# A hybrid encoder block on one Trainium2 core: attention scores and outputs issued as blocks, weight casts put behind evictions, transposes placed later

## The chip, the cores and the metric

The kernel runs on one core of a Trainium2 chip. The metric is the device time of one execution in microseconds (us); three runs of the kernel before were taken, and their median is used. A core has a matrix engine (TensorE, "PE" in the profile; its weight loads are listed apart as "PEld"), a vector engine (DVE), a scalar engine (ACT), a general engine (POOL) and an engine that mostly issues transfers (SP). Each works through its own instructions in the order in which the program gives them, and waits on semaphores for the others.

## The reference

One layer of a hybrid streaming encoder, on 256 tokens of 1024 channels, in fp32: a feed-forward block (FFN), a mixer with two branches (HGRN2, a gated linear recurrence, and FoX, an attention with a forget gate), a read of a 256-token memory by four heads, and a second FFN. Cut to its core:

```python
h = rmsnorm(x, ffn1_pre_g);  x = x + 0.5 * rmsnorm(swiglu(h, ffn1_w_in, ffn1_w_down), ffn1_post_g)

h = rmsnorm(x, mix_pre_g)
q_a, f_a, i_a, g_a, q_b, k_b, v_b, f_b, gates = split(h @ w_in)
o_a = hgrn2_chunkwise(q_a, f_a, i_a, lb)            # recurrence, chunks of 64 tokens
o_a = rmsnorm(o_a, hg_norm_g) * silu(g_a);  y_a = o_a @ w_branch_a
o_b = fox_attention(q_b, k_b, v_b, f_b + bias)      # causal softmax, 128-query blocks
y_b = o_b @ w_branch_b
gate = sigmoid(gates + b_gate)
y = gate[0] * y_a + gate[1] * y_b
x = x + rmsnorm(y @ w_out, mix_post_g)

h = rmsnorm(x, mem_pre_g);  mem_n = rmsnorm(mem, mem_kv_g)
p = softmax(q @ k.T / 16)                           # q = h @ w_mq; k, v = split(mem_n @ w_mkv)
x = x + rmsnorm((p @ v) @ w_mo, mem_post_g)

h = rmsnorm(x, ffn2_pre_g);  x = x + 0.5 * rmsnorm(swiglu(h, ffn2_w_in, ffn2_w_down), ffn2_post_g)
```

## The kernel before

Everything is computed in products of fp32 parts. A weight unit of 128 x 1024 comes in by DMA as `raw`; `load_split` (lines 127 to 136) makes of it `hi` (a cast to fp32r on ACT, line 134) and `lo` (the rest, `raw - hi`, on DVE, line 135). Activations are held transposed in a `Pair` of the same two parts, `hT` and `lT`. A product is three matmuls per block: hi x hi, hi x lo, lo x hi. All matmuls are issued by the helper `MM` on line 90, so most rows of the profile carry that line, and are told apart by their tiles: `mm` (projections, 2 PSUM buffers), `acc` (accumulators, 4 buffers), `tr` (transposes and some small products, 2 buffers). `raw` has 4 buffers, `hi` and `lo` 8 each.

The stages follow each other in program order: FFN 1 (0 to 192 us in the profiled execution), the projections of the mixer with the recurrence (to 344), scores of FoX, its values v_b, outputs and gates, and the two branches (344 to 470), w_out (to 492), the memory read (to 599), FFN 2 (to 785). FFN and projections go through the weights in units of 4 per chunk; tokens come in two halves `h` of 128, and channels in blocks `kb` of 128.

A token-major result becomes a `Pair` through `to_T` (from line 279): eight transposes on PE into two `tr` buffers, four in each, and for every 128 x 128 block an eviction on ACT (`hT`, line 275) and one on DVE (`lT`, line 276). `half` does this for the normed `xs` of one half of the tokens. `split` (lines 152 to 154) makes the two parts from a PSUM tile without a gain.

The order of the engines' work is the program's order, but for blocks under `with after(i)`: they are given a high priority and may be issued only after the i-th matmul of the log. So a constant such as `L_IA = 36` says how many matmuls of the current stage go ahead of a block of transposes. `tc.issue_after` with one instruction does the same for a single transfer or cast. In this kernel those constants are:
- `L_ACT`, `L_F1`, `L_F2`: transposes of the FFN's gated activations (`flush`, line 359) and of the next input;
- `L_IA`, `L_MO`: transposes of `xs` for the second half, in i_a and around the memory output;
- `L_OA`, `F_T`, `F_O`: in the FoX stage, the transposes of the gated HGRN2 output `Gt` into the pair `OA` among v_b, the transposes of the probabilities (`fox_pT`, line 885) and the two outputs (`fox_out`);
- `M_O`: the first two memory outputs.

In the FoX stage the scores of both groups `g` of four heads come first (`fox_scores(0)`, `fox_scores(1)`), then the values, then the first chunk of gates, among which the transposed probabilities and the outputs are placed; further gates follow after the norm of the memory. The scores take their PSUM from `tr` (h = 0) and `acc` (h = 1). In the memory read the scores and the transposes of the probabilities stand between `mem_v(0)` and `mem_v(1)`.

The functions that the change touches, with the line numbers of the profile:

Of the kernel before, what the change touches and what calls it, by code (L numbers as in the profile page):

```python
# [11 lines left out]
F32 = mybir.dt.float32  # L12
F32R = mybir.dt.float32r
I32 = mybir.dt.int32
AF = mybir.ActivationFunctionType
# [3 lines left out]
P = 128  # L19
# [14 lines left out]
STAG = 3  # L34

L_ACT = 21
L_F1 = 24
L_IA = 36
L_WO = 28
L_MK = 108  # L40
L_MO = 21
L_F2 = 44
L_OA = 20
F_T = (8, 26)
F_O = (27, 42)
L_Y = 16
M_O = (24, 36)

R_AT = (52, 126, 210, 254, 298, 344)

# [25 lines left out]
def block_kernel(ctx: ExitStack, tc: tile.TileContext, wts, head_in, gf_in, x_in, mem_in, memT_in, cols, rows, fbias, masks, out):  # L76
# [23 lines left out]
    def nm(s):  # L100
        count[0] += 1
        return f"{s}_{count[0]}"
# [13 lines left out]
    def trp():  # L116
        return pp.tile([P, 512], F32, tag="tr", name=nm("tr"), bufs=2)
# [2 lines left out]
    cache = {}  # L120
    loads = []

    def parts_of():
        return [wp.tile([P, D], F32R, tag=t, name=nm(t), bufs=8) for t in ("hi", "lo")]

    def load_split(src, n=512):

        raw = wp.tile([P, D], F32, tag="raw", name=nm("raw"), bufs=4)
        hi, lo = parts_of()
        r, h, l = raw, hi, lo  # L130
        if n < 512:
            r, h, l = (p.rearrange("p (k n) -> p k n", k=2)[:, :, :n] for p in (raw, hi, lo))
        loads.append(nc.sync.dma_start(r, src).ins)
        S.copy(h, r)  # L134
        V.tensor_tensor(out=l, in0=r, in1=h.bitcast(F32), op=ALU.subtract)  # L135
        return hi, lo

    def unit(name, i):
# [5 lines left out]
    def chunk(name, c):  # L144
        return [unit(name, 4 * c + i) for i in range(4)]
# [4 lines left out]
        return hi[:, o : o + n], lo[:, o : o + n]  # L150

    def split(hi, lo, src):
        S.copy(hi, src)
        V.tensor_tensor(out=lo, in0=src, in1=hi.bitcast(F32), op=ALU.subtract)

    class Pair:

# [112 lines left out]
    def gain_split(X, kb, src, g, a=0, b=T, first=False):  # L270
        gs = cols_s[:, g + kb : g + kb + 1] if isinstance(g, int) else g
        if first:
            V.tensor_scalar(out=X.hi(kb, a, b), in0=src, scalar1=gs, scalar2=None, op0=ALU.mult)
        else:
            S.activation(X.hi(kb, a, b), src, AF.Copy, scale=gs)  # L275
        V.scalar_tensor_tensor(out=X.lo(kb, a, b), in0=src, scalar=gs, in1=X.hi(kb, a, b).bitcast(F32), op0=ALU.mult, op1=ALU.subtract)  # L276

    def to_T(X, src, h, g, qs=(0, 1)):

# [64 lines left out]
    def ffn(w_in, w_dn, X, r2, n_tok, i_row, first_half, second_half=None):  # L344
# [48 lines left out]
        def down(c, h, cols=((0, 512), (512, 1024))):  # L393
            act = acts[c]
            hs = slice(h * P, (h + 1) * P)
            for j in range(2):
                wh, wl = unit(w_dn, 2 * c + j)
                ah, al = act[:, 0, j, hs], act[:, 1, j, hs]
                for lo, up in cols:
                    for i, (a, w) in enumerate(((ah, wh), (ah, wl), (al, wh))):  # L400
                        MM(accs[h][lo // 512][:, lo % 512 : lo % 512 + up - lo], a, w[:, lo:up], start=(c == 0 and j == 0 and i == 0), stop=(c == NFF - 1 and j == 1 and i == 2))
# [19 lines left out]
        for c in range(n_tok, NFF):  # L421
            acts[c] = m4([P, 2, 2, T], F32R, "act")
            if c == 2 and first_half:
                n = len(log)
                (outs,) = act_first((c,), mm)
                for h in range(2):
                    flush(n + L_ACT + 24 * h)
                    act_evac(outs[h], c, h)
            else:
                for h in range(2):  # L430
                    n = len(log)
                    act_tok(c, h)
                    if c == 2 or c > NFF - STAG + 1:
                        flush(n + L_ACT)
            if c == 6:
                grow = load_row(i_row)
                if first_half:
                    with tc.issue_after(loads[-1]):
                        nc.sync.dma_start(masks_s, masks)
            if accs is None:  # L440
                accs = [[acc(), acc()], [acc(), acc()]]
            while done < min(c - 1, NFF - STAG):
                n = len(log)
                for h in range(2):
                    down(done, h)
                flush(n + L_ACT)
                done += 1
        left, right = (0, 512), (512, 1024)
        m = len(log)
        for cut in (left, right):  # L450
            for c in range(NFF - STAG, NFF):
                down(c, 0, (cut,))
        flush(m + L_ACT)
        post(accs[0], 0, grow, 0.5, not first_half)
        m = len(log)
        if first_half:
# [69 lines left out]
    for h in range(2):  # L526
        m = len(log)
        for c in range(2):
            ps = mm()
            proj_tok(ps, X2, chunk("i_a", c), h)  # L530
            iv_last = S.activation(iv[c][:, h, :], ps, AF.Copy, scale=r2[h]).ins
        if h == 0:
            half(X2, r2, 1, G_MIX, m + L_IA, into=fac_of(0, 1))
# [313 lines left out]

    ps_, pT0s, pT1s = {}, [], []

    def fox_scores(g):  # L850
        k, q = kb_[g], qb_[g]
        for h in range(2):
            ns = P * (h + 1)
            if h == 0:
                pv = trp().rearrange("p (i s) -> p i s", i=4)
                pv = [pv[:, i] for i in range(4)]
                p = sp.tile([P, 4, P], F32, tag="z2", name=nm("p0"), bufs=3)
            else:
                pv = score_psum()
                p = m4([P, 4, T], n="p1")  # L860
            mx, sm = s1(4, name="mx"), s1(4, name="sm")
            for i in range(4):
                MM(pv[i], q[:, i, h * P : (h + 1) * P], k[:, i, :ns], start=True, stop=True)
            for i in range(4):
                hd = 4 * g + i
                c1 = ct[:, h * 8 + hd : h * 8 + hd + 1]
                if h == 1:
                    V.scalar_tensor_tensor(out=p[:, i, 0:P], in0=pv[i][:, 0:P], scalar=c1, in1=cbc[:, hd], op0=ALU.add, op1=ALU.subtract)
                ds_ = slice(h * P, (h + 1) * P)
                V.scalar_tensor_tensor(out=p[:, i, ds_], in0=pv[i][:, ds_], scalar=c1, in1=cbm[g][:, i, ds_], op0=ALU.add, op1=ALU.subtract)  # L870
            V.tensor_reduce(out=mx, in_=p, axis=AX.X, op=ALU.max, negate=True)
            for i in range(4):
                S.activation(p[:, i], p[:, i], AF.Exp, bias=mx[:, i : i + 1], accum_out=sm[:, i : i + 1])
            V.reciprocal(sm, sm)
            V.tensor_tensor(out=p, in0=p, in1=bc(sm, [P, 4, ns], 2), op=ALU.mult)
            ps_[g, h] = p

    def fox_pT(g):
        pT0 = m4([P, 4, T], n="pT0")
        pT1 = sp.tile([P, 4, P], F32, tag="pT1", name=nm("pT1"), bufs=1)  # L880
        for h in range(2):
            for b in range(h + 1):
                tr = trp()
                for i in range(4):
                    PE.transpose(tr[:, i * P : (i + 1) * P], ps_[g, h][:, i, b * P : (b + 1) * P], ident)  # L885
                trv = tr.rearrange("p (i s) -> p i s", i=4)
                if b == 0:
                    S.copy(pT0[:, :, h * P : (h + 1) * P], trv)
                else:
                    V.tensor_copy(pT1, trv)  # L890
        pT0s.append(pT0)
        pT1s.append(pT1)
# [13 lines left out]
            i2 = slice(2 * j, 2 * j + 2)  # L906
            split(OB.h[g][:, i2], OB.l[g][:, i2], po.rearrange("p (a t) -> p a t", a=2))

    fox_scores(0)
    fox_scores(1)  # L910
    for c in range(2):
        u = chunk("v_b", c)
        t = m4([P, 2, 512], n="v_b")
# [2 lines left out]
            proj_tok(ps, X2, u, h)  # L916
            S.activation(t[:, h, :], ps, AF.Copy, scale=r2[h])
        vb_.append(t)
    for h in range(2):
        with after(len(log) - L_OA * (2 - h)):  # L920
            to_T(OA, lambda kb: Gt[h][:, kb * P : (kb + 1) * P], h, G_HG)


    zs = []
# [12 lines left out]

    m = len(log)
    gates(0)
    for g in range(2):  # L940
        with after(m + F_T[g]):
            fox_pT(g)
        with after(m + F_O[g]):
            fox_out(g)


# [10 lines left out]
        rm.append(rstd_x([ms[:, 0:512], ms[:, 512:]], fac_of(1, h)))  # L957

    rowm = row_of(fac[1])
    for c in range(1, 4):  # L960
        gates(c)
    for c in (0, 2, 1, 3):
        S.activation(zs[c], zs[c], AF.Sigmoid)
# [74 lines left out]
    def mem_v(c):  # L1038
        u = chunk("mv", c)
        VM.more()  # L1040
        for h in range(2):
# [4 lines left out]
            S.activation(vh, ps, AF.Copy, scale=rm[h])  # L1046
            V.scalar_tensor_tensor(out=vl, in0=ps, scalar=rm[h], in1=vh.bitcast(F32), op0=ALU.mult, op1=ALU.subtract)

    mem_v(0)
    pT = Pair()  # L1050
    for h in range(2):
        a, b = h * P, (h + 1) * P
        sc = s1(name="sc")
        V.tensor_scalar(out=sc, in0=r3[h], scalar1=1.0 / 16.0, scalar2=None, op0=ALU.mult)
# [13 lines left out]
            S.activation(p[:, i], pv[i], AF.Exp, bias=mx[:, i : i + 1], scale=sc, accum_out=sm[:, i : i + 1])  # L1068
        V.reciprocal(sm, sm)
        V.tensor_tensor(out=p, in0=p, in1=bc(sm, [P, 4, T], 2), op=ALU.mult)  # L1070
        for sb in range(2):
            tr = trp()
            for i in range(4):
                PE.transpose(tr[:, i * P : (i + 1) * P], p[:, i, sb * P : (sb + 1) * P], ident)  # L1074
            split(pT.h[sb][:, :, a:b], pT.l[sb][:, :, a:b], tr.rearrange("p (i s) -> p i s", i=4))
    g3 = load_row(2)
    AO = Pair()

# [12 lines left out]
        i2 = slice(2 * (i % 2), 2 * (i % 2) + 2)  # L1091
        split(AO.h[i // 2][:, i2], AO.l[i // 2][:, i2], ps.rearrange("p (a t) -> p a t", a=2))

    m = len(log)
    mem_v(1)
    for i in range(2):
        with after(m + M_O[i]):
            mem_out(i)
    for i in range(2, 4):
        mem_out(i)  # L1100
    X4 = Pair()
    r4 = [None, None]
    po = [[acc(), acc()], [acc(), acc()]]
# [107 lines left out]
```

## Time and profile before

| | |
|---|---|
| Time, median of 3 runs | 794.03 us (793.59 to 794.23) |
| Time of the profiled execution | 793.74 us |
| Its span (first to last recorded instruction) | 791.3 us |
| Mean granted clock of TensorE | 0.998 of full speed |
| Busy DVE, ACT, POOL | 519.0, 426.6, 14.1 us |
| DMA | 147.82 MB, 187 GB/s mean |

Times of the trace count from the start of the span. An instruction of PE counts as busy from its start, also while it waits in the array for its operand, and consecutive matmuls overlap, so lengths of pieces and distances of starts are read, not the sum of durations. "x24" behind a row is the number of instructions in it. A row of the timeline ends with the idle time before it and what released it, where there was any.

### The profile page before, as it was taken

Reading aid. Unit: us, or ns where it says so; the run is one execution under the profiler, and the core shown is the slowest. Engines: PE = TensorE matmul, PEld = TensorE weight load, DVE = VectorE, ACT = ScalarE, POOL = GpSimd, SP = SyncE. Lnnn points to the kernel's source line nnn. Section 1 sums busy time; section 2 is a strip of 40 time slices with the busy share of each in tenths; the row PEclk is TensorE's granted clock in tenths of the full one; section 3 lists DMA queues with packets and bytes.
Section 4 is the critical chain, followed back from the end, with each engine's and each line's share of the span. In section 5 each row is a group of like instructions: output and inputs, shape, how many; then the busy total and the mean of one; then the engine's idle time right before and its main releaser. Section 6 shows DMA issues by size and latency. Waiting matters only on the chain.

```text
span 791.3 us, 12219 instructions
## 1 busy us (share of the span) xinstructions
PE 783.2 (99%) x4736; PEld 678.0 (86%) x4736; DVE 519.0 (66%) x826; ACT 426.6 (54%) x656; POOL 14.1 (2%) x36
## 2 busy tenths in 40 slices
PE   9999999999999999999999999999999999999996
PEld 7888888887899999998888888999888888888885
DVE  6775545557767899498685666966649754545543
ACT  7654444546754667368674345645637644444541
POOL 0000000000000102100000000000000000000000
PEclk9999999999999999999999999999999999999999
DMA  9786654554554547735576654556433656654521
GB/s 349 251 259 203 231 191 160 190 208 161 165 188 143 181 134 224 257 121 173 168 257 222 212 188 161 166 191 201 144 122 133 227 196 207 214 194 159 186 80 54
DMA packets 44345, 147.82 MB, mean 187 GB/s; under 512 B 5048, under 2 KB 8768, under 8 KB 44288
## 3 DMA queue, kind: packets, MB, share of 16 engines
q1 hardware_dynamic: 43168, 144.83, 54.1%
q0 software_dynamic: 688, 1.85, 0.9%
q8 instruction: 37, 0.61, 0.3%
q10 hardware_dynamic: 432, 0.37, 0.1%
q14 instruction: 20, 0.16, 0.1%
HBM read 145.97 MB, written 1.06 MB: 186 GB/s over the span
## 4 chain that ended last, share of the span: by engine, by line
PE 97%; DVE 1%; issue 0%; DMA 0%; ACT 0%; DVEq 0%; ACTq 0%
PE mm L90 67%; PE acc L90 27%; PE tr L359 1%; PE tr L284 1%; PE tr L90 1%; DMA head<-in_head_dram 0%; PE tr L885 0%; DVE lo L135 0%; PE tr L972 0%; PE tr L1074 0%; DVE xs L340 0%; ACT hi L134 0%; DVE G L831 0%; DVE q_b L789 0%; DVE post L330 0%
## 5 line engine op out<-in xcount | busy, mean ns | idle before, releaser
L135 DVE TENSOR_TENSOR lo<-raw,hi 128x1024 fp32r<-128x1024 f32 (+1 forms) x256 | 306.4, 1206 | 124.2 <-ACT hi L134 115.5
L134 ACT CAST hi<-raw 128x1024 fp32r<-128x1024 f32 (+1 forms) x256 | 262.4, 1038 | 151.5 <-PE mm L90 86.5
L90 PE MATMUL mm<-lo,hT 128*128 128x512 f32 (+1 forms) x592 | 227.1, 386 | 0.0
L90 PE MATMUL mm<-hi,hT 128*128 128x512 f32 (+1 forms) x592 | 226.8, 385 | 0.0
L90 PE MATMUL mm<-hi,lT 128*128 128x512 f32 (+1 forms) x592 | 226.3, 386 | 0.0
L90 PEld LDWEIGHTS mm<-hi,hT 128*128 128x128 f32 x592 | 111.2, 188 | 21.9 <-ACT hT L275 0.6
L90 PEld LDWEIGHTS mm<-hi,lT 128*128 128x128 f32 x592 | 111.1, 188 | 21.8 <-DVE lT L276 0.5
L90 PEld LDWEIGHTS mm<-lo,hT 128*128 128x128 f32 x592 | 111.0, 188 | 20.5
L90 PE MATMUL acc<-hi,act 128*128 128x512 f32 x352 | 111.9, 390 | 0.0
L90 PE MATMUL mm<-hT,lo 128*128 128x256 f32 x384 | 109.0, 284 | 0.0
L90 PE MATMUL mm<-hT,hi 128*128 128x256 f32 x384 | 108.9, 284 | 0.0
L90 PE MATMUL mm<-lT,hi 128*128 128x256 f32 x384 | 108.8, 283 | 0.0
L90 PEld LDWEIGHTS acc<-hi,act 128*128 128x128 f32 x352 | 66.0, 188 | 13.1
L90 PEld LDWEIGHTS mm<-hT,hi 128*128 128x128 f32 x384 | 73.6, 192 | 0.1
L90 PEld LDWEIGHTS mm<-lT,hi 128*128 128x128 f32 x384 | 73.6, 192 | 0.1
L90 PEld LDWEIGHTS mm<-hT,lo 128*128 128x128 f32 x384 | 73.6, 192 | 0.1
L90 PE MATMUL acc<-lo,act 128*128 128x512 f32 x176 | 70.0, 398 | 0.0
L364 ACT ACTIVATE sg<-mm,rstd 128x256 f32<-128x256 f32 x40 | 19.0, 475 | 75.9 <-PE mm L90 75.9
L369 DVE SCALAR_TENSOR_TENSOR at<-mm,rstd,sg 128x256 f32<-128x256 f32 x40 | 19.2, 480 | 57.4 <-ACT sg L364 57.4
L90 PEld LDWEIGHTS acc<-lo,act 128*128 128x128 f32 x176 | 33.1, 188 | 6.2
L90 PE MATMUL acc<-hi,hT 128*128 128x512 f32 x96 | 35.5, 398 | 0.4 <-ACT hi L498 0.3
L90 PE MATMUL acc<-hi,lT 128*128 128x512 f32 x96 | 35.2, 394 | 0.0
(199 smaller groups left out, 657.2 us busy)
## 6 DMA issues: line engine op xcount, KB each, us to landing
raw<-in_wts_dram SPq DMA_DIRECT2D x247, 512.0 KB, 4.4
raw<-in_gf_dram SPq DMA_DIRECT2D x12, 344.0 KB, 3.8
head<-in_head_dram SPq DMA_DIRECT2D x7, 392.0 KB, 6.6
grow<-in_rows_dram SPq DMA_DIRECT2D x4, 512.0 KB, 5.8
xs<-in_x_dram SPq DMA_DIRECT2D x2, 512.0 KB, 7.8
cbm<-cd POOLq DMA_DIRECT2D x2, 512.0 KB, 9.2
brow<-in_rows_dram SPq DMA_DIRECT2D x4, 256.0 KB, 5.2
memT<-in_memT_dram SPq DMA_DIRECT2D x2, 512.0 KB, 7.9
```

The costliest lines, as they stand in the source:

```text
L90: log.append(PE.matmul(*args, **kw).ins)
L134: S.copy(h, r)
L135: V.tensor_tensor(out=l, in0=r, in1=h.bitcast(F32), op=ALU.subtract)
L284: PE.transpose(ps[:, j * P : (j + 1) * P], src(kb), ident)
L359: PE.transpose(trv[:, j, h * P : (h + 1) * P], ats[c, h][:, j * P : (j + 1) * P], ident)
L364: silu = S.activation(sg, ps[:, :FC], AF.Silu, scale=r2[h])
L369: V.scalar_tensor_tensor(out=a, in0=ps[:, FC:], scalar=r2[h], in1=sg, op0=ALU.mult, op1=ALU.mult)
```

## The change

Orders and places change; the computation does not.
- FFN: the transposes of the last gated activation are issued as one group of four, after 9 of the last down matmuls, instead of two and two.
- i_a: the casts and `lo` of its second chunk are issued behind the evictions of the first half of X2 (`behind`, `evicted`), and the transposes of the second half after 40 matmuls instead of 36.
- FoX: the scores move from before v_b to its first chunk, after 12 matmuls, both groups for h = 0 and then both for h = 1. The transposes of `Gt` move from the end of v_b into the first gates. The second chunk of gates moves ahead of the memory's norm; the transposes of the probabilities and both outputs are placed among it. `pT1` takes a buffer of the pool "extra".
- Memory: the scores move into `mem_v(0)`, the transposes of the probabilities into `mem_v(1)`, into `acc` PSUM; the outputs follow later in it. The casts of the first four units of `mo` are issued behind the evictions of the probabilities.

```diff
 L_ACT = 21
+L_LAST = 8
 L_F1 = 24
-L_IA = 36
+L_IA = 40
 L_WO = 28
 L_MK = 108
-L_MO = 21
+L_MO = 22
 L_F2 = 44
-L_OA = 20
-F_T = (8, 26)
-F_O = (27, 42)
+L_OA = (4, 24)
+F_S = 12
+F_T = (46, 66)
+F_O = 88
 L_Y = 16
-M_O = (24, 36)
+M_S = (6, 18)
+M_T = (106, 119)
+M_O = (134, 138)

...
+    evicted = [None, None]
+    behind = []
+
     def parts_of():
...
         loads.append(nc.sync.dma_start(r, src).ins)
-        S.copy(h, r)
-        V.tensor_tensor(out=l, in0=r, in1=h.bitcast(F32), op=ALU.subtract)
+        with tc.issue_after(behind[0]) if behind else nullcontext():
+            S.copy(h, r)
+        with tc.issue_after(behind[1]) if behind else nullcontext():
+            V.tensor_tensor(out=l, in0=r, in1=h.bitcast(F32), op=ALU.subtract)
         return hi, lo
...
     def split(hi, lo, src):
-        S.copy(hi, src)
-        V.tensor_tensor(out=lo, in0=src, in1=hi.bitcast(F32), op=ALU.subtract)
+        a = S.copy(hi, src)
+        b = V.tensor_tensor(out=lo, in0=src, in1=hi.bitcast(F32), op=ALU.subtract)
+        return a.ins, b.ins

...
         else:
-            S.activation(X.hi(kb, a, b), src, AF.Copy, scale=gs)
-        V.scalar_tensor_tensor(out=X.lo(kb, a, b), in0=src, scalar=gs, in1=X.hi(kb, a, b).bitcast(F32), op0=ALU.mult, op1=ALU.subtract)
+            evicted[0] = S.activation(X.hi(kb, a, b), src, AF.Copy, scale=gs).ins
+        evicted[1] = V.scalar_tensor_tensor(out=X.lo(kb, a, b), in0=src, scalar=gs, in1=X.hi(kb, a, b).bitcast(F32), op0=ALU.mult, op1=ALU.subtract).ins

...
                     act_tok(c, h)
-                    if c == 2 or c > NFF - STAG + 1:
+                    if c == 2 or c > NFF - STAG + 1 and h == 0:
                         flush(n + L_ACT)
...
             for c in range(NFF - STAG, NFF):
+                if c == NFF - 1 and cut == left:
+                    flush(m + L_LAST)
                 down(c, 0, (cut,))
-        flush(m + L_ACT)
         post(accs[0], 0, grow, 0.5, not first_half)
...
             ps = mm()
-            proj_tok(ps, X2, chunk("i_a", c), h)
+            if h == 0 and c == 1:
+                behind.extend(evicted)
+            u = chunk("i_a", c)
+            behind.clear()
+            proj_tok(ps, X2, u, h)
             iv_last = S.activation(iv[c][:, h, :], ps, AF.Copy, scale=r2[h]).ins
...
-    def fox_scores(g):
-        k, q = kb_[g], qb_[g]
-        for h in range(2):
+    def fox_scores(h):
+        for g in range(2):
+            k, q = kb_[g], qb_[g]
             ns = P * (h + 1)
...
-    def fox_pT(g):
+    def fox_pT(g, m):
         pT0 = m4([P, 4, T], n="pT0")
-        pT1 = sp.tile([P, 4, P], F32, tag="pT1", name=nm("pT1"), bufs=1)
-        for h in range(2):
-            for b in range(h + 1):
-                tr = trp()
+        pT1 = wp.tile([P, D], F32, tag="extra", name=nm("pT1"), bufs=4)[:, :512].rearrange("p (i s) -> p i s", i=4)
+        for h, b in ((0, 0), (1, 0), (1, 1)):
+            tr = trp()
+            with after(m + 5 * b):
                 for i in range(4):
...
-    fox_scores(0)
-    fox_scores(1)
+    m = len(log)
     for c in range(2):
...
         vb_.append(t)
-    for h in range(2):
-        with after(len(log) - L_OA * (2 - h)):
-            to_T(OA, lambda kb: Gt[h][:, kb * P : (kb + 1) * P], h, G_HG)
+        if c == 0:
+            for h in range(2):
+                with after(m + F_S):
+                    fox_scores(h)

...
     gates(0)
+    for h in range(2):
+        with after(m + L_OA[h]):
+            to_T(OA, lambda kb: Gt[h][:, kb * P : (kb + 1) * P], h, G_HG)
     for g in range(2):
-        with after(m + F_T[g]):
-            fox_pT(g)
-        with after(m + F_O[g]):
+        fox_pT(g, m + F_T[g])
+    gates(1)
+    for g in range(2):
+        with after(m + F_O):
             fox_out(g)
...
     rowm = row_of(fac[1])
-    for c in range(1, 4):
+    for c in range(2, 4):
         gates(c)
...
+    m = len(log)
     mem_v(0)
     pT = Pair()
-    for h in range(2):
+    pm, marks = {}, {}
+
+    def mem_scores(h):
         a, b = h * P, (h + 1) * P
...
         V.tensor_tensor(out=p, in0=p, in1=bc(sm, [P, 4, T], 2), op=ALU.mult)
+        pm[h] = p
+
+    def mem_pT(h):
+        a, b = h * P, (h + 1) * P
+        p = pm[h]
         for sb in range(2):
-            tr = trp()
+            tr = acc()
             for i in range(4):
                 PE.transpose(tr[:, i * P : (i + 1) * P], p[:, i, sb * P : (sb + 1) * P], ident)
-            split(pT.h[sb][:, :, a:b], pT.l[sb][:, :, a:b], tr.rearrange("p (i s) -> p i s", i=4))
+            marks[h] = split(pT.h[sb][:, :, a:b], pT.l[sb][:, :, a:b], tr.rearrange("p (i s) -> p i s", i=4))
+    for h in range(2):
+        with after(m + M_S[h]):
+            mem_scores(h)
     g3 = load_row(2)
...
-    m = len(log)
     mem_v(1)
+    for h in range(2):
+        with after(m + M_T[h]):
+            mem_pT(h)
     for i in range(2):
...
         mem_out(i)
+
+    for kb in range(4):
+        behind.extend(marks[kb // 2])
+        unit("mo", kb)
+        behind.clear()
     X4 = Pair()
```

## The prediction

> **What bounds the kernel now.** I read the profile page first, then the chain that ended last in order of time, then the timeline around each place where a piece of that chain is longer than its count of instructions allows.
>
> ```profile
> PE 783.2 (99%) x4736; PEld 678.0 (86%) x4736; DVE 519.0 (66%) x826; ACT 426.6 (54%) x656; POOL 14.1 (2%) x36
> ...
> PE 97%; DVE 1%; issue 0%; DMA 0%; ACT 0%; DVEq 0%; ACTq 0%
> ```
>
> The first line is busy time by engine, the second the share of the chain that ended last. TensorE is the bound and nearly the whole chain. A change that leaves its instructions as they are can only win the time in which it stands still, and "99%" hides that time: an instruction that waits for its operand in the array counts as busy. So I read stalls from the chain's pieces (start, length, engine, tile, line, count):
>
> ```profile
> 173.09 0.22 PE tr L359 x2
> ...
> 175.15 0.26 PE tr L359 x2
> ...
> 191.35 3.10 PE mm L90 x13
> 194.48 5.75 PE mm L90 x24
> 200.23 0.44 PE tr L284 x4
> ...
> 344.30 0.76 DVE G L831
> 345.11 1.99 PE acc L90 x8
> ...
> 350.31 1.73 PE acc L90 x8
> ...
> 381.13 0.70 PE acc L90 x2
> ...
> 382.38 0.43 PE acc L90 x2
> ...
> 391.16 53.97 PE mm L90 x238
> ...
> 445.56 5.47 PE mm L90 x24
> ...
> 596.03 0.63 PE tr L284 x4
> ...
> 769.04 0.37 PE tr L359 x2
> ```
>
> The yardsticks are the undisturbed pieces: 24 wide matmuls in 5.47 us, so 0.228 us each (238 in 53.97 says 0.227); four transposes 0.44; two 0.22; eight score matmuls 1.73; a pair of fox_out matmuls 0.43. Against them:
> - A, i_a: 13 in 3.10 instead of 2.96, 24 in 5.75 instead of 5.47: 0.42 us lost.
> - B, fox scores: eight in 1.99 instead of 1.73: 0.26, behind DVE's G on line 831.
> - C, fox_out: a pair in 0.70 instead of 0.43: 0.27.
> - E, transposes of xs near 596: 0.63 instead of 0.44: 0.19.
> - F, FFN tails: 0.26 and 0.37 instead of 0.22 each: 0.19.
>
> Two losses need the timeline of PE (start, length, then the instruction):
>
> ```profile
> 343.82 1.17 PE L90 MATMUL tr<-k_b,q_b 128*128 128x128 f32 x9
> 345.11 1.13 PE L90 MATMUL acc<-k_b,q_b 128*128 128x256 f32 x4
> ...
> 571.84 0.40 PE L90 MATMUL mm<-hi,lT 128*128 128x512 f32 x1
> 572.33 0.50 PE L90 MATMUL acc<-hi,hT 128*128 128x512 f32 x1
> 572.66 0.39 PE L90 MATMUL acc<-lo,hT 128*128 128x512 f32 x1
> 572.89 0.39 PE L90 MATMUL acc<-hi,hT 128*128 128x512 f32 x1
> ```
>
> At B PE also stands still from 344.99 to 345.11, so B is 0.38. At D (the first matmuls with the mo weights, behind the first memory output) starts are 0.49 and 0.33 apart instead of 0.23: 0.36.
>
> Together 0.42 + 0.38 + 0.27 + 0.36 + 0.19 + 0.19 = 1.81 us. That is all this change can reach; start and end of the kernel (first loads, last norm, output) it does not touch. The profiled execution took 793.74 us, 2.4 outside its span of 791.3; the median of the runs is 794.03. I sum against 793.74 and move the result by the 0.3 between them. A measurement of this kernel can tell about 0.2% (1.6 us) from no change, so even the whole 1.81 barely counts as faster.
>
> **What is removed.** The set of PE, DVE, ACT and DMA instructions stays; only orders move, and a few switches between wide matmuls and transposes fall away. By the new order all six should go.
> A: the ACT casts of i_a's second chunk leave the gap between evictions of X2:
>
> ```profile
> 193.09 1.07 ACT L134 CAST hi<-raw 128x1024 fp32r<-128x1024 f32 x1
> 194.03 0.66 ACT L275 ACTIVATE hT<-tr,cols_s 128x128 fp32r<-128x128 f32 x2
> ...
> 196.04 1.22 DVE L135 TENSOR_TENSOR lo<-raw,hi 128x1024 fp32r<-128x1024 f32 x1
> ...
> 198.97 1.41 DVE L311 SCALAR_TENSOR_TENSOR xs<-post,y,xs 128x512 f32<-128x512 f32 x2
> ```
>
> The evictions at 194.03, whose columns the piece of 24 needs, start behind a 1.07 us cast; without it they would be early by more than the 0.42. B: scores start 13 matmuls (2.96 us) later, when G, which ended 0.05 before 345.11, is long done. C: pT transposes and fox_out are 3 to 8 matmuls apart instead of one. D: the mo product has more wide matmuls between output blocks, and its casts no longer precede the evictions. E: one matmul more, 0.23 of cover against 0.19. F: nine matmuls ahead of four transposes instead of 2+2; the at tiles are then ready with under 0.1 us to spare.
>
> **What new waits cost.** Each moved step meets other work.
>
> *i_a, half 1.* DVE's lo on line 135 (1.22 us) of that chunk now follow the evictions, ahead of xs (line 311), which feeds the next transposes. xs ended at 200.38; walking DVE's new order with these durations, it ends near 201.1. PE wants its second four at 200.23 − 0.42 + 4 × 0.228 + 0.44 = 201.16. Nearly a tie; I take 0.2. Bounds: nothing, or one lo more ahead of xs, 1.2 less 0.1 = 1.1.
>
> *Transposes of the gated output among gates(0), of the probabilities among gates(1).* They share two PSUM buffers ("tr"). With gates(1) pulled ahead, the sigmoid of gates(0), with its table load, falls among evictions of the gated output's half 1 on ACT.
>
> ```profile
> 376.37 1.61 ACT L275 ACTIVATE hT<-tr,cols_s 128x128 fp32r<-128x128 f32 x4 [0.42 <-DVE lT L276]
> ...
> 378.66 0.58 ACT L888 COPY pT<-tr 128x512 f32<-128x512 f32 x1
> ...
> 392.39 1.05 ACT L134 CAST hi<-raw 128x1024 fp32r<-128x1024 f32 x1 [0.61 <-PE mm L90]
> 393.46 1.28 ACT L963 ACT_TABLE_LOAD   x1
> 394.75 1.06 ACT L963 ACTIVATE zg<-zg 128x1024 f32<-128x1024 f32 x1
> 397.31 2.91 ACT L275 ACTIVATE hT<-memT,cols_s 128x256 fp32r<-128x256 f32 x7 [1.49 <-DMA memT<-in_memT_dram]
> ```
>
> On DVE the gate's eviction:
>
> ```profile
> 379.13 0.75 DVE L935 SCALAR_TENSOR_TENSOR zg<-mm,fac,brow 128x512 f32<-128x512 f32 x1
> ```
>
> From the start of half 1's first block, PE is back for that block's buffer after two times (0.44 + 11 × 0.228) = 5.9 us. The buffer is free after 0.44 (transposes), 0.1 hand-over, two evictions 0.65, table load and sigmoid 1.28 + 1.06 = 2.34, five evictions at 1.61/4 = 0.40, so 2.0, and DVE's last half about 0.5: 6.0. So 0.1 of wait. Then pT blocks are only 3 matmuls (0.68) apart, each buffer needs a copy of 0.58 and a hand-over: two more waits near 0.1. After a wait PE loses about another 0.1 (at D the second start was 0.10 late too). Three waits at 0.2: 0.6. Bounds: nothing if I am 0.1 too pessimistic on each, 1.0 if DVE's gate eviction, which waits for PE ahead of these evictions, comes late as well.
>
> The table load stands 0.02 after the end of the cast, and the sigmoid starts 0.01 after the load ends: 1.28 us is its whole price here. [...]
>
> *Loads.* On SP the broadcast row of gates(1) now stands earlier and memT and br_a's loads behind a row whose buffer waits for fox_out. In the row at 397.31 ACT already waited 1.49 us for memT while PE ran its 238 matmuls from 391.16 without a stall, so a few us more there cost nothing. I take nothing; the bound is 1 us, if br_a's weights behind them came that late.
>
> *Memory.* Scores move into mem_v(0); pm transposes go to "acc" PSUM inside mem_v(1), and casts of the first mo units wait for their evictions.
>
> ```profile
> 561.22 1.07 ACT L153 CAST hT<-tr 128x512 fp32r<-128x512 f32 x2 [3.63 <-PE tr L1074]
> ...
> 561.83 1.29 DVE L154 TENSOR_TENSOR lT<-tr,hT 128x512 fp32r<-128x512 f32 x2 [2.78 <-ACT hT L153]
> ```
>
> A block of mem_out holds its "tr" buffer until both casts are done: about 0.55 on ACT, 0.65 on DVE, and up to two lo (2.4) that now stand on DVE ahead of it: 3.6. PE is back for it after 4 + 5 wide matmuls (2.05) and twelve of a half block (12 × 0.12 = 1.44, half the length of a wide one): 3.5. I take two waits, together 0.3; bounds nothing and 1.3 (one lo more).
>
> **The sum.** −1.81 + 0.2 + 0.6 + 0.3 = −0.7 us. Against 793.74: 793.0; on the median's scale 793.3. Bounds: −1.8 with every new wait covered, and −1.81 + 1.1 + 1.0 + 1.3 = +1.6 with all three at their ends.
>
> **Rivals.**
> 1. All new waits are covered (each is within 0.3 us of fitting): −1.8 us, 792.2, faster. For it: the 0.1 margins are as small as my error in them. Against: five of them must all fall right.
> 2. Slower: ACT stands at the sigmoid, with the evictions of the gated output queued behind it. The sigmoid needs the second half of gates(0) from DVE, an eviction of 0.75 us that PE finishes feeding only just before half 1's first block. DVE works in order: if two lo (1.22 each, 2.4) get ahead of that eviction, the sigmoid starts 2.4 late, the first buffer comes free 2.4 late, and blocks 0.68 apart cannot win it back, since each needs a copy of 0.58: −0.7 + 2.4 + 0.3 = +2.0, so 796.0. It decides at the end of that eviction: harmless up to the moment when ACT has loaded its table (about 2.2 us after the block's start), PE pays one for one behind it. For it: a waiting engine in order, and 0.1 of margin behind it. Against: by the new order the nearest lo stands behind that eviction, not ahead of it.
> 3. The held-back casts do not leave the gap (the order was the same in the engine before PE needed it), or the same wait returns elsewhere: A and D stay, −1.81 + 0.78 + 0.9 = −0.1, 793.9: no change.
> 4. A second stand-still of ACT as long as the load itself (1.28 us, row at 393.46), at the switch to the sigmoid: the buffer comes free 1.3 later, −0.7 + 1.3 = +0.6, 794.6: no change either. [...] The rows at 392.39 to 394.75, back to back, speak against it.
>
> **How the numbers follow.** My forecast with small deviations 0.40, rival 3 with mixtures that cancel 0.10, rival 4 0.03, rival 1 and near it 0.26, rival 2 and other late transfers 0.21. Faster by over 0.2% needs below 792.4, which only rival 1 reaches: 0.26. Slower needs above 795.6: 0.21. Within: 0.53. Predicted 793.3. The range goes from 791.9 (rival 1 with 0.3 for what I may misread in the stalls) to 795.6 (the +1.6 of those upper bounds); above it lies most of rival 2.
>
> **What would show it.** In the changed profile: the pieces of the chain in i_a should be 0.228 per matmul; the first score matmuls should follow without a gap; the pair of 0.70 should be 0.43; the four transposes near 596 should be 0.44. New waits should stand where I put them: at line 885's transposes (the "tr" buffer), at the transposes of xs for i_a's half 1, at the first mo matmuls. [...] If TensorE's busy work itself differs by over 0.5 us in undisturbed stretches, my premise that order costs nothing is wrong.

## The result and the profile after

The changed kernel takes 792.28 us (median of 13 runs, 791.92 to 792.69), the kernel before 794.15 us (13 runs): 1.87 us less, a ratio of 0.9978 with a 95% interval of 0.9971 to 0.9986. The ratio is 0.22% below 1, a little more than the 0.2% that the prediction took as the least that can be told, and its interval reaches to both sides of that; the forecast was 793.3, no change.

The gain has two parts, and only one of them stands in the trace. The profiled execution after took 792.24 us with a span of 790.4. So the span is 0.9 shorter than the 791.3 before, and what lies outside the span fell from 2.44 to 1.84 us. The medians agree: the span is 791.5 us over the 98 runs of the kernel before that were taken with the experiments, and 790.5 over the 13 of the changed one; time less span is 2.47 and 1.79. But single runs of the kernel before scatter in this: 92 of them lie between 2.32 and 2.64 us, six between 2.06 and 2.12.

**Inside the span.** Each stage can be timed by itself, between pieces of the chain that ended last which both kernels have: the transposes of xs ahead of i_a, of zf ahead of the FoX stage, of the gates, of xs in the memory read, and the gated activations of FFN 2. Lines of the source have moved: 90 is now 94, 134 and 135 are 142 and 144, 275 and 276 are 285 and 286, 284 is 294, 885 is 900, 888 is 903. Before, from the chain in order of time:

```profile
187.96 0.87 PE tr L284 x8
...
292.43 0.22 PE tr L765 x2
...
445.12 0.43 PE tr L972 x4
...
495.64 0.44 PE tr L284 x4
...
626.41 0.44 PE tr L359 x4
...
739.05 0.44 PE tr L359 x4
...
784.65 0.02 issue
```

And after:

```profile
188.03 0.87 PE tr L294 x8
...
191.43 9.30 PE mm L94 x41
200.72 0.87 PE tr L294 x8
...
292.00 0.22 PE tr L780 x2
...
349.94 1.73 PE acc L94 x8
...
388.69 0.53 PE tr L900 x4
389.22 0.69 PE mm L94 x3
389.91 0.97 PE tr L900 x8
...
391.58 0.97 PE tr L900 x8
...
393.25 0.66 PE tr L900 x4
...
444.53 0.44 PE tr L991 x4
...
495.04 0.44 PE tr L294 x4
...
571.69 0.35 PE tr L94 x3
572.05 0.69 PE acc L94 x3
572.74 0.74 PE tr L94 x5
...
594.98 0.94 PE tr L294 x8
...
597.53 10.46 PE mm L94 x45
...
625.60 0.44 PE tr L369 x4
...
738.24 0.44 PE tr L369 x4
...
783.77 0.02 issue
```

| stage, from landmark to landmark | before | after | difference | forecast |
|---|---|---|---|---|
| i_a and the recurrence (xs to zf) | 104.47 | 103.97 | −0.50 | −0.2 |
| FoX and gates (zf to zg) | 152.69 | 152.53 | −0.16 | −0.05 |
| memory and start of FFN 2 (xs to at) | 130.77 | 130.56 | −0.21 | −0.25 |
| end of FFN 2 (at to the last matmul) | 45.60 | 45.53 | −0.07 | −0.15 |
| end of FFN 1 | | | −0.04 | −0.04 |

Together −0.98; the start-up of this execution was 0.11 longer, which leaves the 0.9 of the spans. A stage without an edit repeats within 0.10 us from one profiled execution to another (one exception is named at b_act3). So i_a is clear, memory and FFN 2 are at about twice the noise or less, and the FoX difference needs the repeats: the stage without its edit took 152.69 here but 152.62 to 152.65 in five other kernels, and with the edit 152.48 to 152.53 in five. That makes about 0.12 instead of 0.16.

What to see in the pieces: i_a runs 41 matmuls in 9.30, 0.227 each, and eight transposes in 0.87: stall A is gone and no new one came. The score matmuls take 1.73 everywhere. But FoX's transposes of probabilities take 0.53, 0.97, 0.97 and 0.66 where 0.44, 0.87, 0.87 and 0.44 would be undisturbed: 0.51 us. And in the transposes of xs at 594.98, where stall E was, 0.07 is left, but the next piece of 45 wide matmuls takes 10.46 instead of 10.27. The kernel before has, for the first four transposes of this place and for those 45 matmuls:

```profile
595.49 0.52 PE tr L284 x4
...
598.51 10.27 PE mm L90 x45
```

So 0.19 was given back within the next 3 us. (The first four lost 0.08 before as well; the prediction counted E from the second four alone.)

**Outside the span.** In its profiled execution the kernel before fetches one more block of its program 2.3 us after its last recorded instruction. The list of DMA queues (packets, MB, share) in the window from 791 to 800 us, the span having ended at 791.3, is for the kernel before:

```profile
q14 instruction: 1, 0.01, 0.3%
```

The profile of the changed kernel has no packet behind its span. Nothing in the diff speaks of this.

### The profile page after: what moved, and what is told of

The parts are those of the page before. It is cut to its first block, busy times and chain, and to the rows that moved or that the text cites. A ratio compares the mean times of both kernels' runs of the same rounds, so it can differ in the third digit from the quotient of the medians.

```text
span 790.4 us, 12205 instructions
## 1 busy us (share of the span) xinstructions
PE 782.3 (99%) x4736; PEld 677.6 (86%) x4736; DVE 519.2 (66%) x826; ACT 426.7 (54%) x656; POOL 13.4 (2%) x36
## 4 chain that ended last, share of the span: by engine, by line
PE 98%; DMA 1%; DVE 0%; ACT 0%; issue 0%; SPq 0%; DVEq 0%; ACTq 0%
PE mm L94 67%; PE acc L94 27%; PE tr L369 1%; PE tr L94 1%; PE tr L294 1%; DMA head<-in_head_dram 1%; PE tr L900 0%; PE tr L991 0%; PE acc L1101 0%; DVE xs L350 0%; DVE post L340 0%; ACT hi L509 0%; SPq L493 0%; ACT hT L285 0%; SPq L488 0%
## 6 DMA issues: line engine op xcount, KB each, us to landing
head<-in_head_dram SPq DMA_DIRECT2D x7, 392.0 KB, 6.5
```

## The experiments

**The four parts alone.** Each is the kernel before with one part of the diff (the same lines as in the diff above) and the constants that belong to it.

```diff
 only_ffn: +L_LAST = 8   and the two hunks at flush()
 only_ia:  -L_IA = 36 +L_IA = 40   and behind.extend(evicted) around chunk("i_a", 1)
 only_fox: the hunks from fox_scores to gates, L_OA, F_S, F_T, F_O
 only_mem: the hunks from mem_v to mo, M_S, M_T, M_O, -L_MO = 21 +L_MO = 22
```

> The kernel before with the FFN part alone (transposes of the last gated activation as one group of four after nine down matmuls, in both FFNs). Theory 1 (the time went where the chain of the changed kernel is shorter): stall F goes, 0.04 in FFN 1 and 0.08 to 0.15 in FFN 2, so 0.1 to 0.2 us less, both in the time and in the span. Theory 2 (about 0.6 us of the measured gain of 1.9 lies outside the span and comes with one part, whichever it is): if this is the part, the time is 0.7 to 0.8 less while the span is 0.1 to 0.2 less. Rival 3 of the prediction (the wait returns elsewhere): nothing.

> The kernel before with the i_a part alone (casts and lo of its second chunk behind the evictions, transposes of half 1 after 40 matmuls). By the prediction's sum 0.42 less and 0.2 more, so 0.2 less; if the new wait at the transposes of xs stays away, as the chain of the changed kernel suggests, 0.4 to 0.5 us less, in time and span alike. If the part outside the span comes with it, the time is 1.0 less. Rival 3: nothing.

> The kernel before with the FoX part alone (scores inside v_b, transposes of the gated output inside gates(0), of the probabilities and the outputs inside gates(1)). By the prediction's sum 0.65 less and 0.6 more: 0 to 0.1 less; the chain of the changed kernel says 0.16 less. If all new waits were covered: 0.65 less. If the part outside the span comes with it: 0.7 less, with a span 0.1 to 0.2 shorter. Rival 2 would show a piece longer by over 1 us at line 885's transposes: it is not expected any more.

> The kernel before with the memory part alone (scores inside mem_v(0), transposes of the probabilities inside mem_v(1) in acc PSUM, casts of the first mo units behind their evictions, transposes of xs one matmul later). By the prediction's sum 0.55 less and 0.3 more, 0.25 less; the chain of the changed kernel says 0.39 less up to the second half's transposes and 0.17 given back behind them, so 0.2 less. If the part outside the span comes with it, 0.8 less with a span 0.2 shorter.

Measured, beside 793.85 us of the kernel before on the same chip (33 runs; 11 runs of each part):

| part | time | ratio, 95% | span, median | time less span | its own stage |
|---|---|---|---|---|---|
| before | 793.85 | | 791.4 | 2.46 | |
| FFN | 793.78 | 0.9998 (0.9989 to 1.0007) | 791.4 | 2.48 | −0.12 and −0.04 |
| i_a | 792.88 | 0.9989 (0.9981 to 0.9998) | 791.1 | 1.80 | −0.50 |
| FoX | 793.17 | 0.9995 (0.9986 to 1.0003) | 791.3 | 1.82 | −0.17 |
| memory | 793.02 | 0.9989 (0.9980 to 0.9998) | 791.2 | 1.79 | −0.25 |

"Its own stage" is read as in the table above, from the profiled execution of each part; for i_a and FoX the rows are:

```profile
188.37 0.87 PE tr L290 x8
...
292.34 0.22 PE tr L775 x2
```

```profile
294.14 0.22 PE tr L772 x2
...
446.66 0.44 PE tr L983 x4
```

that is 103.97 and 152.52. Two things follow. In their own stages the parts do what they do together, within the 0.10 of repeats, so no sign of work on each other is seen. And the 0.65 outside the span comes with any of three parts, not with one and not with a sum: theory 2 as it was put falls. It is the same 1.8 after one edit or after four, so what switches seems to belong to the program as a whole.

The fetch behind the span does not follow the kernel so simply. The FFN part has 2.48 as its median, but its profiled execution is one of four with 2.06 to 2.10 (the other seven have 2.38 to 2.60), and its profile shows no fetch behind the span. In the FoX part nine runs have 1.77 to 1.87 and two have 2.37 and 2.39. So the time outside the span has three levels, near 1.8, 2.1 and 2.5, and a kernel can take two of them.

**What switches the time outside the span.** Idle copies were added, which make no stage faster. Both were written into the middle of FFN 2.

```diff
 b_dve1 (kernel before)            b_act3 (kernel before)
                 grow = load_row(i_row)
+                if not first_half:
+                    V.tensor_copy(idle[:, 0:128], ident)      # b_dve1, once
+                    S.copy(idle[:, 0:128], ident)             # b_act3, three times
```

> The kernel before with one idle 128x128 copy more on DVE, in the middle of FFN 2, where DVE has time; nothing else changes. It asks what the time outside the span (time less span: 2.46 us for the kernel before and for the FFN part alone, 1.80 for the other three parts and for all) depends on. Theory A, the lengths of the engines' programs, by DVE's: 1.80, and the time falls by 0.65 us although work was added. Theory B, by ACT's length: stays at 2.46. Theory C, a property of what the edits do to the work: stays at 2.46. The span should not move by more than 0.1 in any.

> The kernel before with three idle 128x128 copies more on ACT, in the middle of FFN 2. Theory A (DVE's program length sets the time outside the span): stays at 2.46. Theory B (ACT's): 1.80, time lower by 0.65. Theory C (a property of the work): 2.46. The span unmoved within 0.1.

b_dve1: 793.88 us (8 runs), span 791.3, outside 2.50: unchanged. The trace counts as many instructions on DVE as before (1118), because with the copy one waiting instruction fell away; so this run says nothing on theory A. Its profile has the fetch behind the span again (2.3 us behind, in an execution with 2.55 outside); of its eight runs five have 2.48 to 2.60 and three 2.07 to 2.09. b_act3: 793.77 us (8 runs), outside 1.82, while the span grew to 791.95. The three copies went not where they were meant to but into the start-up (as did the one of b_dve1, at 10.3 us):

```profile
L439 ACT COPY idle<-ident x1: 284/284/284, 9.4 to 9.4; 128x128 f32<-128x128 f32 x1
```

(line, engine, operation: ns at least, median, at most; first and last start in us). The span grew by 0.45 us, and of that 0.35 stands in the stage of i_a, which took 104.82 in the profiled execution although it has no edit. The time outside the span fell by 0.64 all the same. So theory C is refuted as it was put: work added for nothing switches it too. That points at the program as it is laid out, not at what the change is about. The reverse was tried on the changed kernel:

```diff
 a_act4 (changed kernel)
+                        with tc.issue_after(evicted[0]):
+                            S.copy(idle, ident)             # four times, FFN 2
```

> The changed kernel with four idle 128x128 copies more on ACT behind the last evictions of X4 at the start of FFN 2, so that the trace counts 951 instructions on ACT as for the kernel before. So far the time outside the span was 2.46 us where it counts 951 (kernel before, FFN part alone, one more copy on DVE) and 1.80 where it counts 947, 949 or 954. Theory B (the length of ACT's program): 2.46 again, so 0.65 us more in the time than in the span, and in the profile a fetch of instructions behind the end of the span, as the kernel before has one 2.3 us behind it. Theory C (a property of the edits): 1.80. The copies are about 1.1 us of ACT, so the span may grow by up to that if evictions or casts there have no slack.

792.26 us (8 runs), span 790.45, outside 1.84. But the count on ACT came to 950, not 951, for a waiting instruction fell away here too, so theory B was not put to the test. Over all kernels the trace counts on ACT 951 in the three with medians of 2.46 to 2.50 us, and 946, 947, 949, 950 or 954 in the eleven with 1.78 to 1.84. That agrees with theory B, that the length of ACT's program decides, but it is not shown: no kernel was brought back to 951. Nor is the fetch behind the span the whole of it. Two profiles of kernels with 951 have it, in executions with 2.44 and 2.55 us; the third, of the FFN part, has none at 2.07, which is still 0.27 above 1.80. So the fetch may be the step from 2.1 to 2.5; what makes the step from 1.8 to 2.1 is open.

**Rival 2 made on purpose.**

```diff
 a_slow (changed kernel), at the sigmoid of zs[c]
+        with tc.high_priority() if c == 0 else nullcontext():
+            for i in range(2 if c == 0 else 0):
+                S.activation(zs[c], zs[c], AF.Copy)
             S.activation(zs[c], zs[c], AF.Sigmoid)
```

The edit does one thing more than its text below says: the passes and the sigmoid are also given a high priority.

> The changed kernel with two more passes of 1.06 us of ACT over the gates' first chunk ahead of its sigmoid, so that ACT holds the evictions of the gated output 2.1 us longer: rival 2 made on purpose. The forecast's margin at the first tr buffer was 0.1: PE should then stand still about 2 us at the first transposes of the probabilities (line 885 of the kernel before), one for one, and not win it back: time +2 us or a little more (later copies wait too). If the buffer had slack that the sum missed: less than 1 us.

792.32 us (8 runs), span 790.5: nothing lost. Its chain:

```profile
389.83 0.36 DVE lT L286
...
390.24 0.66 PE tr L900 x4
390.89 1.38 PE mm L94 x6
```

The buffer did come free at 390.2, 1.6 us later than in the changed kernel, and the transposes of probabilities came with it. But the program came out in another order: more matmuls of gates(1) stand ahead of the block, and six instead of three between the blocks. So PE had work, and the stage (zf to zg) took 152.59 against 152.48 to 152.53. The price that rival 2 names was therefore not tested in the old order. What the run shows is that two passes more on ACT with a high priority gave an order in which matmuls fill the time instead of a stall; whether the priority or the added work made that order is not shown.

**The waits at the "tr" buffers.**

```diff
 a_sig (changed kernel)
+        with tc.issue_after(pT_done[0]) if c == 0 else nullcontext():   # last S.copy of fox_pT
             S.activation(zs[c], zs[c], AF.Sigmoid)
```

> The changed kernel with the sigmoid of the gates' first chunk (and its table load, together 2.34 us) issued behind the last copy of transposed probabilities on ACT. By the prediction's sum the three waits at the tr buffers (0.04, 0.09, 0.10, 0.10 and 0.22 in the chain of the changed kernel, 0.55 together) lose the part that comes from the evictions: 0.1 to 0.3 us less. If they come only from the copies of 0.59 that free the buffers with 0.69 between the blocks: nothing. If the sigmoid is then late for the branch product at 444: a new stall there; it has about 50 us, so none is expected.

792.12 us (11 runs), ratio to the kernel before 0.9978 (0.9969 to 0.9987), span 790.3. The blocks of probabilities:

```profile
388.79 0.44 PE tr L901 x4
389.22 0.69 PE mm L94 x3
389.91 0.97 PE tr L901 x8
...
391.59 0.96 PE tr L901 x8
...
393.25 0.66 PE tr L901 x4
```

The first wait is gone (0.44 instead of 0.53) with 2.34 us of ACT out of its way. The other three stay as they were. PE's weight loads there wait three times, each time for a copy `pT` on ACT (us in total, times, longest):

```profile
PEld tr L901 <- ACT pT L904: 1.0, 3, 0.4
```

So these waits come from the copies, 0.59 each, that must free two buffers between blocks 0.69 apart. The longest of them, 0.22, has a cast in it as well: in the changed kernel's trace, the copy that it waits for starts on ACT at 392.62 behind a cast that started at 391.66 and takes 1.05, while the transposes to be copied were done at about 392.0. What that wait would be without the cast was not tried. The stage took 152.39, about 0.1 less than in the five executions with the changed FoX stage; the ratio of the times, 0.9978, is the same as for the changed kernel, so the time can't show it.

**i_a with its old place for half 1.**

```diff
 a_ia36 (changed kernel)
-L_IA = 40
+L_IA = 36
```

> The changed kernel with the transposes of half 1 in i_a placed after 36 matmuls, as in the kernel before, and the casts still behind the evictions. In the changed kernel xs ended at 200.53 and PE's second four transposes came at about 201.0. Four matmuls earlier they come at 200.1: if xs decides, PE waits about 0.4 us there and the segment i_a loses most of its gain of 0.5. If the gain comes from the casts alone and xs has more slack: no change. By the forecast's own estimate (xs at 201.1) it would be 0.9.

792.58 us (8 runs), span 790.8: 0.3 more. In its chain PE now waits for xs:

```profile
201.19 0.76 DVE xs L321
...
201.99 0.66 PE tr L294 x4
202.65 0.24 PE mm L94
202.89 0.44 PE tr L294 x4
```

(in this execution the work ahead began 2.1 us later than in the changed kernel's). Four transposes take 0.66 instead of 0.44, and the stage gains 0.17 instead of 0.50. So the four matmuls more are needed to keep the gain. xs itself ends only 0.15 later than in the kernel before (200.53 and 200.38); PE comes 0.42 earlier, since stall A is gone, and four matmuls (0.91) give xs the time. The other half, 40 matmuls with the casts in their old place, was not run.

**Where E went, and the best version.**

```diff
 a_f2 (changed kernel), in act_tok
+            if not first_half and c == 1 and h == 0:
+                behind.extend(evicted)          # for units 2 and 3 of the chunk only
 a_both: a_sig and a_f2
```

> The changed kernel with the casts of the last two units of FFN 2's second chunk issued behind the evictions of X4's first half. In the changed kernel PE waits 0.17 us at 598.5 for an eviction that stands on ACT behind such a cast, just where the transposes of xs one matmul later should have won 0.19. If that cast is the cause: 0.1 to 0.2 us less, in the span. If the squares of the last norm, which stand there too, are the cause, or the held casts come late for the second chunk (needed from about 606): no change, or up to 0.5 more.

> The changed kernel with both extensions: sigmoid of the gates' first chunk behind the last copy of transposed probabilities, casts of FFN 2's second chunk behind the evictions. If they add up: the 0.16 us measured for the first and 0.1 to 0.2 for the second, so 0.25 to 0.35 less than the changed kernel, 791.9 to 792.0 on the scale where the kernel before takes 793.94. The time outside the span should stay at 1.80 if ACT's count is not 951.

a_f2: 792.09 us (10 runs), span 790.3. The piece of 45 matmuls behind the transposes of xs:

```profile
597.53 10.32 PE mm L94 x45
```

It is 10.32 here and 10.34 in a_both; the six kernels with the memory part and without this edit have 10.40 to 10.46. So the cast, with its `lo` on DVE that the edit moves too, was the cause of about 0.1 of the 0.13 to 0.19 lost. The squares of the norm still stand ahead of the eviction on ACT, which starts at 598.24 instead of 598.37. a_both: 792.00 us (10 runs), ratio to the kernel before 0.9975 (0.9966 to 0.9985), span 790.2, FoX stage 152.40, memory stage 130.44. The time cannot tell it from the changed kernel (the intervals overlap). By the stages FoX is about 0.1 better (152.48 to 152.53 without the edit). The memory stage, 130.44 as in a_f2, is hardly outside what five kernels without that edit have, 130.46 to 130.56, so only the piece of 45 shows that gain.

## Why the prediction was right and where it was off

The direction was right, the time within the range, the likeliest case not: 792.28 is almost the 792.2 of rival 1, but rival 1 isn't what happened: the new waits that it excludes are there. That the time comes so near to it is chance, for a third of the gain comes from outside the span.

- **All that can be won is the stalls, 1.81.** For the span this held: the gain there is 0.9 to 1.0, and the undisturbed pieces run as before (0.227 per wide matmul). The total gain of 1.87 is above that ceiling. The step that failed is the one that took the 2.4 us outside the span as given; 0.65 us, a third of the gain, came from there, and no row of the profile before had been asked about it. Why it came is open. Without that the time would have been about 792.9, 0.4 from the forecast.
- **i_a, −0.42 + 0.2.** Measured −0.50. The term mis-sized is the new wait at xs: the walk through DVE's new order ended at 201.1, the trace has xs end at 200.53, so the tie was half a microsecond of slack and the wait was nothing. That a wait stood this near was right: four matmuls earlier it is there. DVE in the changed kernel:

```profile
193.67 1.23 DVE L144 TENSOR_TENSOR lo<-raw,hi 128x1024 fp32r<-128x1024 f32 x1
...
197.34 1.22 DVE L144 TENSOR_TENSOR lo<-raw,hi 128x1024 fp32r<-128x1024 f32 x1
...
199.12 1.41 DVE L321 SCALAR_TENSOR_TENSOR xs<-post,y,xs 128x512 f32<-128x512 f32 x2
```

Between the first row and the second stand two more lo and three small operations of the norm (0.15, 0.22 and 0.16). Three lo alone are 3.67, which is the distance of the two starts: the small operations cost almost nothing there, and a walk that adds up all lengths comes out 0.5 too late.
- **FoX, −0.65 + 0.6.** Measured −0.16 (−0.12 by the repeats), with 0.51 us of waits at the place that was named, in four pieces instead of three. The first was put down to the evictions and the others to the copies; a_sig shows the first, and the waits of the weight loads in its trace show the others. The cast ahead of one copy was not in the sum.
- **Rival 4, a second stand-still at the table load.** Neither the trace of the changed kernel nor those of the kernel before and of a_slow (386.40 us: load 0.01 behind the eviction, sigmoid 0.01 behind the load) have one. The changed kernel has the switch among the evictions, where it would have hurt:

```profile
383.31 0.62 ACT L285 ACTIVATE hT<-tr,cols_s 128x128 fp32r<-128x128 f32 x2
383.95 1.28 ACT L982 ACT_TABLE_LOAD   x1
385.24 1.06 ACT L982 ACTIVATE zg<-zg 128x1024 f32<-128x1024 f32 x1
```

Load 0.02 behind the eviction, sigmoid 0.01 behind the load, as behind the cast in the kernel before: the 1.28 us of the load and these 0.03 are all that ACT loses there, so rival 4 did not happen.
- **Memory, −0.55 + 0.3.** Measured −0.21 to −0.25, as summed, but by other terms, so the agreement is luck. The two waits for a `tr` buffer, together 0.3, did not come. At the first mo matmuls 0.14 is left (five short matmuls in 0.74 instead of 0.60), and E's gain was given back at 598.5, which the prediction did not look for. Both times a weight load waited for an eviction on ACT, of the memory's values (L1065) and of X4 (L285):

```profile
PEld mm L94 <- ACT hT L285: 0.3, 1, 0.3
PEld tr L94 <- ACT hT L1065: 0.2, 1, 0.2
```

On the second, one matmul later for the transposes is one matmul later for all that waits for them. And E was 0.08 more than the 0.19 in the list of stalls.
- **FFN tails, −0.19.** Measured −0.11 in the changed kernel and −0.16 alone.
- **Loads, nothing.** This held: behind the outputs 192 matmuls from 400.99 us take 43.54, 0.227 each.
- **Rival 2** did not happen: DVE runs the gates' eviction at 382.75, ahead of its next lo at 383.41, so the condition of this rival was not met. Its price in a fixed order stays untested. **Rival 3** holds for E, and for D with the 0.14 that is left there.

## What to carry to other kernels

When one engine is busy 99% of the span, list its stalls one by one from the pieces of the chain against their undisturbed rate; their sum is an estimate of the most that reordering can win inside the span (here 1.81 us, of which the span gave 0.9 to 1.0), and each new wait can be looked for by name at the buffer or the engine that the moved step shares. Moving a block later moves what waits for its result as well: follow the result to its first reader before counting the gain. And look at time and span apart: the difference between them fell here by about 0.65 us with each of three parts and by 0.64 with three idle copies, so a gain of that size needs an edit that does nothing as a control.

## What the runs showed of the hardware

The time outside the span took medians of about 2.47 or 1.80 us for programs of one and the same kind, and three idle copies were enough to switch it; single runs lie near 1.8, 2.1 or 2.5. In the profiles with 2.44 and 2.55 us a block of instructions is fetched 2.3 us behind the span; in that with 2.07, and in those of the changed kernel (1.84) and b_act3 (1.8), none is. The page of the profile counts 37 fetches of 0.61 MB on one queue and 20 of 0.16 MB on the other, so 16 and 8 KB each:

```profile
q8 instruction: 37, 0.61, 0.3%
...
q14 instruction: 20, 0.16, 0.1%
```

The one behind the span is of the second queue, so 8 KB. Whether the length of an engine's program decides the time outside the span, and which engine's, is open. The start-up varies too: in the chain, the transposes of zf began at 292.00 us in the changed kernel and at 294.40 in a_ia36, whose stage of i_a ahead of them is only 0.33 longer, which is why the stages above are timed between landmarks.
